# A ring of left operands with 2560 bytes a tile instead of 2112, and small tiles in a pool that closes early

## The chip, the cores and the metric

The kernel runs on one core of one Trainium2 chip. The metric is the device time of one execution in microseconds (us). Times that are compared are medians of several executions on the same chip.

## The reference

One decoder block on 1024 tokens of width 1024, in float32: an RMSNorm, one wide projection, two recurrent mixers side by side (a Mamba-2 scan and gated linear attention), a gated merge, cross-attention on 256 memory tokens, a SwiGLU feed-forward part with an inner width of 2816, and a last RMSNorm. Cut to what matters:

```
proj   = rmsnorm(h) @ w_in                     # 1024 x 7712
y_ssd  = ssd_mixer(z, xBC, dt, ...)            # conv, chunked scan, gated norm
y_gla  = gla_mixer(q, k, v, r, a1, ...)
merged = sigmoid(g_ssd) * (y_ssd @ w_up_ssd) + sigmoid(g_gla) * (y_gla @ w_up_gla)
h      = h + merged @ w_o
h      = h + cross_attention(rmsnorm(h), rmsnorm(mem)) # w_xq, w_xkv, w_xo
g, u   = split(rmsnorm(h) @ w_ffn_in, 2)
h      = h + (silu(g) * u) @ w_ffn_out
out    = rmsnorm(h)
```

## The kernel before

Every large product is made in float32r with each operand split in two: `hi` is the rounded value, written by ScalarE, and `lo` is the rest, written by VectorE or GpSimd (`split`, L221). A product is then three matmuls: hi by hi, hi by lo and lo by hi.

The projection and the gate and up halves of the feed-forward part go through `Unit` objects (L275). One unit covers 256 columns of the weight matrix and all tokens, as a two by two block scheme with seven products instead of eight (`B11`, `B21`, `T1`, `B22`, `T2`, `T3`, `T4`). `Unit.step` (L320) makes one of the seven: it takes a 128x512 left block (a block of the raw weights, or a sum of blocks in `sa`), takes a pair of tiles from the ring `wring`, splits the block into them, and issues 12 matmuls, four blocks of the inner dimension by three. In these matmuls the left operand is the stationary one (128x128, loaded into TensorE before the matmul), and the right operand is the moving one (128x512, streamed through). The right operands (`B11h`, `B11l`, `T1h` and so on) are made once by `Operands` (L230) and lie in slots of 8192 bytes a partition in the pools `sl0op` and `sl1aux`; the results `o` and the raw weights lie in such slots too.

```
def wring():                                              # L225
    hi = wp.tile([P, 528], F32R, name="whi", tag="whi", bufs=3)
    lo = wp.tile([P, 528], F32R, name="wlo", tag="wlo", bufs=3)
    return hi, lo
...
for k in range(kh):                                       # in Unit.step, L341
    for x, y in ((wh, xh), (wh, xl), (wl, xh)):
        PE.matmul(p[:, cs], x[:, k, :], y[:, k, cs], ...)
```

The helper's `PE.matmul` stands on L51, so all matmuls carry that line, and all `tensor_tensor` operations of the helpers stand on L73. The first matmul of a list such as (wh, xh), (wh, xl), (wl, xh) has `x` as stationary and `y` as moving operand.

The ring has three tiles `whi` and three `wlo`. A unit uses 512 of a tile's 528 columns. Two other users take them: `kv_unit` (L549) uses 512 columns for the memory keys and values, and `v_steps` (L636) uses all 528, as two blocks of 264 columns, as moving operands.

The other dense products do not use the ring. `dense` (L1176) takes left operands from two slots named `wd` (the five matrices w_up_ssd, w_up_gla, w_o, w_xq, w_xo) and right operands `hl`, all of them in slots. The last stage, with w_ffn_out, takes both operands from slots named `fs`. Attention takes keys and values from slots named `kvhl`.

A tile pool gives each tile a fixed place in SBUF, one pool behind the other: `const`, the ring, the 14 `op` slots, the 4 `aux` slots, two tiles `sa`, and behind these the pools of one stage after the other (`vp` and `stg`; `gprep`; `conv`; `ssd`; `gla`; then the 4 `m` slots, `res` and `sa2`), which take the same room in turn. A tile in that room waits for the last users of what lay there. The scheduler sets the order of instructions; hints of priority (`ahead`) draw the splits and the evacuations of PSUM forward.

The stages in order of time: memory keys and values, x and the v columns (0 to about 200 us); the z columns with the preparation of the scans, then the convolution's units (to about 400); r, q, k and the first gate columns beside the Mamba-2 scan (to about 620); gate columns beside gated linear attention (to about 840); the five dense products with attention (to about 1340); the gate and up units (1350 to 1800); the w_ffn_out product (to the end).

Of the kernel before, what the change touches and what calls it, by code (L numbers as in the profile page):

```python
# [9 lines left out]
F32 = mybir.dt.float32  # L10
F32R = mybir.dt.float32r
# [5 lines left out]
P = 128  # L17
# [4 lines left out]
MEM = 256  # L22
# [7 lines left out]
NCH = TOK // CH  # L30
NH = 16
# [47 lines left out]
def block_kernel(ctx: ExitStack, tc: tile.TileContext, t: dict, out: bass.AP):  # L79
# [10 lines left out]
    def pool(name, bufs=1, space=None, stack=None):  # L90
        kw = {"reuse_waits": "tile"} if space is None else {"space": space}
        return (stack or ctx).enter_context(tc.tile_pool(name=name, bufs=bufs, **kw))

    cp = pool("const")
    dr = pool("dram", 1, bass.MemoryType.DRAM)
    wp = pool("w", 3)
# [42 lines left out]
    def open_slots(key, n, stack):  # L139
        slots[key] = (pool(f"sl{len(slots)}{key}", n, stack=stack), n)  # L140
# [5 lines left out]
    open_slots("op", 14, opst)  # L146
    open_slots("aux", 4, auxst)
    sums = {"aux": pool("sa0", 2, stack=auxst)}

    st1 = ExitStack()  # L150
    vp = pool("vp", 1, stack=st1)
# [54 lines left out]
    def rsqrt(o, v, scale):  # L206

        DVE.tensor_scalar(o, v, scale, EPS, ALU.mult, ALU.add)
        POOL.tensor_tensor(o, o, mhalf[:, :o.shape[1]], ALU.pow)
# [13 lines left out]
        sub(e or DVE, lo, src, hi)  # L223

    def wring():  # L225
        hi = wp.tile([P, 528], F32R, name="whi", tag="whi", bufs=3)
        lo = wp.tile([P, 528], F32R, name="wlo", tag="wlo", bufs=3)
        return hi, lo

    class Operands:  # L230

# [43 lines left out]
    class Unit:  # L275
# [44 lines left out]
        def step(s, name, B, cs=ALL, again=False):  # L320
            s.load()
            kh = s.kh
            if name == "B11":
                s.banks, s.swap, s.u = {}, B.swap, False
                s.out()
            if again:
                wh, wl = s.w
            else:
                with ahead():
                    src = s.left(name)  # L330
                    hi, lo = wring()
                    s.w = wh, wl = [x[:, :kh * P].rearrange("p (k c) -> p k c", c=P) for x in (hi, lo)]
                    split(src, wh, wl)
            xh, xl = B[name]
            key = s.BANK[name]
            fresh = key not in s.banks
            if fresh:
                s.banks[key] = acc()
            p = s.banks[key]
            m = 0  # L340
            for k in range(kh):  # L341
                for x, y in ((wh, xh), (wh, xl), (wl, xh)):
                    PE.matmul(p[:, cs], x[:, k, :], y[:, k, cs], start=fresh and m == 0, stop=m == 3 * kh - 1,
                              skip_group_check=True)
                    m += 1
            s.evac(name, p, cs)
# [106 lines left out]
    def drain(g):  # L453
        for _ in g:
            pass
# [88 lines left out]
    for a in range(2):  # L544
        ACT.activation(msq, wide(mt[:, a]), AF.Square, accum_out=mss[:, a:a + 1])
    rsqrt(mss, mss, 1.0 / D)
    mbc = cp.tile([P, MEM], F32, name="mbc")

    def kv_unit(c0):  # L549

# [6 lines left out]
        for kk in range(4):  # L557
            with ahead():
                hi, lo = wring()
                hv = hi[:, :512].rearrange("p (k c) -> p k c", c=256)  # L560
                lv = lo[:, :512].rearrange("p (k c) -> p k c", c=256)
                split(raw[:, 2 * kk:2 * kk + 2, :], hv, lv, either(lo))
            for i in range(2):
                o = pa[i][:, :256]
                for k2 in range(2):
                    k = 2 * kk + k2
                    for m, (x, y) in enumerate(((hv, mh), (lv, mh), (hv, ml))):
                        w_, m_ = x[:, k2, :], y[:, k, :]
                        if c0 < D:
                            PE.matmul(o, w_[:, i * P:(i + 1) * P], m_, start=k == 0 and m == 0, stop=k == 7 and m == 2)  # L570
                        else:
                            PE.matmul(o, m_[:, i * P:(i + 1) * P], w_, start=k == 0 and m == 0, stop=k == 7 and m == 2)
            yield
# [41 lines left out]
    w_in = t["w_in"]  # L615


    dt_t = cp.tile([P, NCH, NH], F32, name="dt_t")
    a1_t = cp.tile([P, NCH, NH], F32, name="a1_t")
    HW = 264  # L620

    vraw = {}
# [13 lines left out]
    def v_steps():  # L636
        for pr in range(2):
# [13 lines left out]
            for n, name in enumerate(CHAIN):  # L651
                parts = []
                with ahead():
                    e = either(A11, 2.0)
                    if name == "T1":
                        add(e, sa, A21, A22)
                    elif name == "B22":
                        sub(e, sa, sa, A11)
                        sub(either(A11, 2.0), A12, A12, sa)
                    elif name == "T3":  # L660
                        sub(e, A21, A11, A21)
                    a = (A11, A12, sa, A12, sa, A21, A22)[n]
                    for k2 in range(2):
                        hi, lo = wring()
                        hv, lv = hi.rearrange("p (k c) -> p k c", c=HW), lo.rearrange("p (k c) -> p k c", c=HW)
                        split(a[:, 2 * k2:2 * k2 + 2, :], hv, lv)
                        parts.append((hv, lv))
# [46 lines left out]

    st2 = ExitStack()
    gp = pool("gprep", 1, stack=st2)
    cs = cp.tile([P, P], F32, name="cs")
    dec = cp.tile([P, P], F32, name="dec")
    ec = cp.tile([P, P], F32, name="ec")
    dtv = cp.tile([P, NCH, NH], F32, name="dtv")  # L720
    ebm = cp.tile([P, 4, NCH], F32, name="ebm")
    ebl = cp.tile([P, 4, NCH], F32, name="ebl")
    ewl = cp.tile([P, 4, NCH], F32, name="ewl")

    def conv(u, unit):
        cv = cvp.tile([P, 2, TOK], F32, name="cv", tag="cv", bufs=2)
# [377 lines left out]
    run(singles(gs[1:] + gg[:3], B, gg[3:]), (gla, 8 * 5 / 36), prio=PRIO)  # L1104
    drain(gla)
    st4.close()


    st5 = ExitStack()
# [110 lines left out]
    def presum():  # L1220


        r = slot("m", (P, 2, D), name="pre")
        for k in range(KP):
            SP.dma_start(r, t["w_ffn_out"][256 * k:256 * k + 256, :].rearrange("(j p) c -> p j c", p=P))
            yield
            a = lambda i, j: r[:, j, half(i)]
            s1_ = sums["m"].tile([P, HALF], F32, name="sa", tag="sa", bufs=2)
            put = lambda n, ap: SP.dma_start(down_d[(n * KP + k) * P:(n * KP + k + 1) * P, :], ap)
            e = lambda: either(s1_, 1.0)  # L1230
            add(e(), s1_, a(1, 0), a(1, 1))
            put(0, s1_)
            yield
            sub(e(), a(1, 1), s1_, a(0, 0))
            put(1, a(1, 1))
            yield
            sub(e(), a(1, 0), a(0, 0), a(1, 0))
            put(2, a(1, 0))
            yield
            sub(e(), a(0, 1), a(0, 1), a(1, 1))  # L1240
            put(3, a(0, 1))
            yield
# [48 lines left out]
    early = presum()  # L1291
# [301 lines left out]
    for x, (n, k, kn) in enumerate(todo):  # L1593
        name = CHAIN[n]
# [4 lines left out]
        cs = slice(0, 256) if n == 6 else ALL  # L1599
# [9 lines left out]
    cs = slice(256, 512)  # L1609
# [43 lines left out]
```

## Time and profile before

| | |
|---|---|
| time, median of 3 runs | 2020.93 us (2019.97 to 2023.35) |
| profiled execution | 2021.46 us, of which span 2019.7 us |
| mean granted TensorE clock | 0.994 |
| TensorE matmuls | busy 97% of the span |
| VectorE / ScalarE / GpSimd | busy 65% / 43% / 33% |
| DMA | 309.59 MB, mean 153 GB/s |

The span runs from the first to the last instruction. PE stands for TensorE's matmuls and PEld for its loads of stationary operands, which run beside the matmuls; DVE is VectorE, ACT is ScalarE, POOL is GpSimd, SP is the engine whose queue issues the DMAs. Matmuls overlap in the pipeline, and their ends are modelled, so the time of one (about 390 ns in the groups) is a latency. What a matmul costs is the distance from its start to the next one's start. Where the chain of the profile merges a run of matmuls that follow each other without a wait, that distance is the length of the piece divided by the number in it.

### The profile page before, as it was taken

How to read it: one execution, taken by the hardware profiler on the slowest of the kernel's cores; microseconds unless marked ns; L12 is line 12 of the kernel's file. 1: busy time of each engine (PE TensorE's matmuls, PEld its weight loads, DVE VectorE, ACT ScalarE, POOL GpSimd, SP SyncE). 2: the span in 40 equal slices, each digit the busy share in tenths (PEclk: the TensorE clock that was granted, in tenths of full speed). 3: DMA queues.
4: the chain of work that ended last, by engine and by line, in shares of the span. 5: the costliest groups of instructions: out<-in, count | busy, mean ns of one | idle time of the engine just before them, and what ended most of it. 6: DMA issues, size and time to landing. Idle time of an engine off the chain costs nothing.

```text
span 2019.7 us, 26310 instructions
## 1 busy us (share of the span) xinstructions
PE 1951.1 (97%) x9772; PEld 1616.6 (80%) x9772; DVE 1314.3 (65%) x1869; ACT 861.4 (43%) x1482; POOL 658.6 (33%) x482
## 2 busy tenths in 40 slices
PE   7899999999999989999999999999999999999998
PEld 7798678877777778787778888877888888887887
DVE  6866679879986656532444227478777777774565
ACT  7434745465552455432233226453333333354243
POOL 3521343355653212023322100255444444430002
PEclk9899999999999999999999999999999999999999
DMA  9332232356553655797773210433224223276463
GB/s 308 133 117 98 97 121 105 123 180 190 168 168 107 211 160 177 249 356 247 283 238 132 79 42 22 138 126 107 79 89 136 89 82 114 77 258 221 149 228 128
DMA packets 240724, 309.59 MB, mean 153 GB/s; under 512 B 16443, under 2 KB 164133, under 8 KB 240597
## 3 DMA queue, kind: packets, MB, share of 16 engines
q1 hardware_dynamic: 240596, 307.92, 45.6%
q8 instruction: 77, 1.26, 0.3%
q14 instruction: 51, 0.41, 0.1%
HBM read 211.07 MB, written 96.80 MB: 152 GB/s over the span
## 4 chain that ended last, share of the span: by engine, by line
PE 46%; DMA 6%; DVE 4%; issue 3%; ACT 2%; POOL 1%; SPq 0%; POOLq 0%; ACTq 0%; DVEq 0%
PE acc L51 41%; PE bank L51 5%; DMA gates<-gg_d 2%; DMA ysg_d<-gates 1%; PE bank L55 1%; DMA gates<-gs_d 1%; POOL pre L73 1%; DVE fs L73 1%; DMA down_d<-pre 1%; DMA fr<-act_d 1%; DMA pre<-in_w_ffn_out_dram 1%; DVE hl L73 1%; DVE gates L73 1%; DMA hl<-ys_d 0%; POOL ssum L73 0%
## 5 line engine op out<-in xcount | busy, mean ns | idle before, releaser
L51 PE MATMUL acc<-hl,wd 128*128 128x512 f32 x1920 | 442.2, 390 | 8.4 <-ACT wd L222 4.4
L51 PEld LDWEIGHTS acc<-hl,wd 128*128 128x128 f32 x1920 | 359.2, 188 | 87.3 <-ACT wd L222 6.1
L73 DVE TENSOR_TENSOR wlo<-raw,whi 128x512 fp32r<-128x512 f32 x264 | 242.6, 923 | 78.1 <-ACT whi L222 77.8
L222 ACT ACTIVATE whi<-raw 128x512 fp32r<-128x512 f32 x272 | 170.1, 629 | 249.9 <-PE acc L51 223.4
L73 DVE TENSOR_TENSOR o<-acc,o 128x512 f32<-128x512 f32 (+1 forms) x256 | 172.7, 676 | 112.9 <-PE acc L51 99.2
L51 PE MATMUL acc<-fs 128*128 128x512 f32 (+1 forms) x792 | 156.0, 356 | 1.6 <-ACT o L1548 1.5
L51 PEld LDWEIGHTS acc<-fs 128*128 128x128 f32 x792 | 130.6, 189 | 22.7 <-ACT o L1548 1.9
L73 POOL TENSOR_TENSOR raw<-raw,sa 128x512 f32<-128x512 f32 x48 | 65.5, 1364 | 252.9 <-DVE wlo L73 249.7
L222 ACT ACTIVATE fs<-fr 128x1024 fp32r<-128x1024 f32 (+1 forms) x84 | 80.0, 985 | 112.9 <-PE acc L51 39.7
L73 DVE TENSOR_TENSOR fs<-fr,fs 128x1024 fp32r<-128x1024 f32 (+1 forms) x84 | 99.8, 1218 | 38.7 <-ACT fs L222 38.1
L73 DVE TENSOR_TENSOR wd<-raw,wd 128x1024 fp32r<-128x1024 f32 x40 | 50.4, 1261 | 86.8 <-ACT wd L222 86.6
L222 ACT ACTIVATE whi<-sa 128x512 fp32r<-128x512 f32 x96 | 60.0, 626 | 103.5 <-PE acc L51 103.2
L73 POOL TENSOR_TENSOR sa<-raw 128x512 f32<-128x512 f32 x47 | 73.4, 1562 | 84.7 <-DMA raw<-in_w_in_dram 47.3
L73 DVE TENSOR_TENSOR wlo<-sa,whi 128x512 fp32r<-128x512 f32 x96 | 83.1, 865 | 23.6 <-ACT whi L222 22.1
L73 POOL TENSOR_TENSOR raw<-raw 128x512 f32<-128x512 f32 x48 | 82.8, 1725 | 4.9 <-DVE sa L73 4.9
L73 POOL TENSOR_TENSOR ssum<-ssum,sq 128x512 f32<-128x512 f32 (+1 forms) x23 | 35.2, 1532 | 147.5 <-ACT sq L489 143.6
L51 PE MATMUL acc<-B21h,whi 128*128 128x512 f32 x192 | 77.4, 403 | 2.9 <-ACT o L352 2.9
L73 POOL TENSOR_TENSOR o<-o 128x512 f32<-128x512 f32 x29 | 49.3, 1704 | 91.3 <-DVE o L73 81.0
L51 PE MATMUL acc<-B11h,whi 128*128 128x512 f32 x192 | 76.2, 397 | 2.3 <-ACT whi L222 2.3
L51 PE MATMUL acc<-T1h,whi 128*128 128x512 f32 x192 | 76.4, 398 | 1.4 <-ACT whi L222 1.4
L51 PE MATMUL acc<-T2h,whi 128*128 128x512 f32 x192 | 76.2, 397 | 1.5 <-ACT whi L222 1.5
L51 PE MATMUL acc<-T4h,whi 128*128 128x512 f32 x192 | 76.7, 399 | 1.1 <-DVE o L73 1.1
(376 smaller groups left out, 4798.4 us busy)
## 6 DMA issues: line engine op xcount, KB each, us to landing
raw<-in_w_in_dram SPq DMA_DIRECT2D x26, 1024.0 KB, 6.5
raw<-in_w_ffn_in_dram SPq DMA_DIRECT2D x22, 1024.0 KB, 7.7
act_d<-o SPq DMA_DIRECT2D x77, 256.0 KB, 2.3
fr<-act_d SPq DMA_DIRECT2D x35, 512.0 KB, 4.8
pre<-in_w_ffn_out_dram SPq DMA_DIRECT2D x11, 1024.0 KB, 6.0
fr<-down_d SPq DMA_DIRECT2D x20, 512.0 KB
down_d<-pre SPq DMA_DIRECT2D x33, 256.0 KB, 3.3
raw<-in_w_xkv_dram SPq DMA_DIRECT2D x8, 1024.0 KB
```

Of the source, the lines that this page charges most:

```text
L51: return s.e.matmul(o, x, y, **kw)
L55: return s.e.transpose(o, x, i)
L73: return f(*a, **kw)
L222: ACT.activation(hi, src, AF.Copy)
```

## The change

The ring's tiles become 640 columns wide, 2560 bytes a partition, of which the kernel uses the first 528 as before. Ten small tiles (`mbc`, `dt_t`, `a1_t`, `cs`, `dec`, `ec`, `dtv`, `ebm`, `ebl`, `ewl`, together 4480 bytes) move from the pool `const`, which stays for the whole kernel and lies ahead of the ring, to a new pool `early` behind `sa`, which is closed when gated linear attention is done.

```
-        hi = wp.tile([P, 528], F32R, name="whi", tag="whi", bufs=3)
-        lo = wp.tile([P, 528], F32R, name="wlo", tag="wlo", bufs=3)
-        return hi, lo
+        return [wp.tile([P, 640], F32R, name=n, tag=n, bufs=3)[:, :528] for n in ("whi", "wlo")]
...
     sums = {"aux": pool("sa0", 2, stack=auxst)}
+    st_early = ExitStack()
+    ep = pool("early", 1, stack=st_early)
...
-    mbc = cp.tile([P, MEM], F32, name="mbc")
+    mbc = ep.tile([P, MEM], F32, name="mbc")
...
-    cs = cp.tile([P, P], F32, name="cs")
+    cs = ep.tile([P, P], F32, name="cs")
...
     drain(gla)
     st4.close()
+    st_early.close()
```

The other eight small tiles change from `cp.tile` to `ep.tile` in the same way. In the built programs the tiles begin at these bytes of a partition (behind the stroke the rest on division by 512):

| | before | after |
|---|---|---|
| whi | 9696/480, 11808/32, 13920/96 | 5216/96, 7776/96, 10336/96 |
| wlo | 16032/160, 18144/224, 20256/288 | 12896/96, 15456/96, 18016/96 |
| slots op, aux, m | all rest 352 | all rest 96 |
| sa, first stage pool | rest 352, 173920/352 | rest 96, 176608/480 |

A step of `k` in a unit is 512 bytes in the left operand and 2048 in the right one, so the rests hold for all 12 matmuls of a product. In the tiles of `v_steps` the second block of 264 columns begins 1056 bytes, 32 more than twice 512, behind the first.

Every engine's instructions are the same and stand in the same order before and after. The waits differ in a few instructions where the dense products begin.

More of the change, by code (lines that the diff above doesn't have):

```diff
@@ L615, in block_kernel @@
     w_in = t["w_in"]
-    dt_t = cp.tile([P, NCH, NH], F32, name="dt_t")
-    a1_t = cp.tile([P, NCH, NH], F32, name="a1_t")
+    dt_t = ep.tile([P, NCH, NH], F32, name="dt_t")
+    a1_t = ep.tile([P, NCH, NH], F32, name="a1_t")
     HW = 264
@@ L716, in block_kernel @@
     gp = pool("gprep", 1, stack=st2)
-    cs = cp.tile([P, P], F32, name="cs")
[L718 to L723, printed above, removed]
+    cs = ep.tile([P, P], F32, name="cs")
+    dec = ep.tile([P, P], F32, name="dec")
+    ec = ep.tile([P, P], F32, name="ec")
+    dtv = ep.tile([P, NCH, NH], F32, name="dtv")
+    ebm = ep.tile([P, 4, NCH], F32, name="ebm")
+    ebl = ep.tile([P, 4, NCH], F32, name="ebl")
+    ewl = ep.tile([P, 4, NCH], F32, name="ewl")
     def conv(u, unit):
```

## The prediction

> **What bounds the kernel now.** I read the busy shares first, then a table of 100 us stretches, then the chain of work that ended last, and last the waits of TensorE's matmuls stage by stage. The page's first part has an engine's busy time, its share of the span and its instructions:
>
> ```profile
> PE 1951.1 (97%) x9772; PEld 1616.6 (80%) x9772; DVE 1314.3 (65%) x1869; ACT 861.4 (43%) x1482; POOL 658.6 (33%) x482
> ```
>
> TensorE is the engine to watch, but being busy 97% only says that it rarely has nothing in flight. The stretches show whether another engine is near its own limit where the ring is used (two of the scan, one of the convolution, one of the gate and up units; start:end, length, then busy time of each engine, clock and DMA share):
>
> ```profile
> core 0: us, PE busy (x) PEld busy (x) DVE busy (x) ACT busy (x) POOL busy (x), PEclk, DMA share, GB/s
> 300.00:400.00 100.00, 100.00 (x431) 80.30 (x431) 90.96 (x93) 50.59 (x66) 37.90 (x22) 1.00 0.33 114
> 400.00:500.00 100.00, 96.67 (x606) 77.62 (x605) 83.81 (x143) 55.93 (x125) 50.35 (x39) 1.00 0.59 183
> 500.00:600.00 100.00, 96.54 (x620) 78.81 (x619) 86.10 (x154) 55.93 (x125) 59.65 (x45) 1.00 0.60 181
> 1400.00:1500.00 100.00, 100.00 (x433) 81.06 (x432) 74.75 (x94) 34.12 (x59) 45.36 (x31) 1.00 0.34 111
> ```
>
> TensorE has the full clock in all four and work in flight nearly all the time; VectorE is next, closest at 91% in the convolution. So here the rate at which matmuls start sets the pace. The chain gives that rate, since it merges matmuls that follow each other without a wait (start, length, count):
>
> ```profile
> 1032.72 103.20 PE acc L51 x454
> ...
> 1139.68 68.62 PE acc L51 x302
> ...
> 1273.34 72.77 PE acc L51 x321
> ...
> 1387.80 391.98 PE acc L51 x1691
> ...
> 1849.99 50.09 PE bank L51 x221
> ```
>
> All are float32r matmuls of 128x512. The first three pieces are dense products (`wd` by `hl`): 103.20/454 = 227.3 ns, 68.62/302 = 227.2, 72.77/321 = 226.7. The last is the w_ffn_out product (`fs` by `fs`): 226.7. Together 294.68/1298 = 227.0 ns. The fourth is the gate and up stage, all of it ring products: 391.98/1691 = 231.8 ns. Shape and clock are the same, and no wait of the matmul queue falls in these pieces. The difference is 4.8 ns a matmul, 2.1%.
>
> What differs is where the operands lie. In the four fast pieces both come from slots, with the same rest 352 at 512 bytes; in the slow piece the left one comes from the ring with the rests 480, 32, 96, 160, 224 and 288. Which two operands meet, the timeline shows (start, length):
>
> ```profile
> 1500.07 0.39 PE L51 MATMUL acc<-T2h,wlo 128*128 128x512 f32 x1
> 1500.08 0.19 PEld L51 LDWEIGHTS acc<-T2h,whi 128*128 128x128 f32 x1
> ...
> 1500.30 0.39 PE L51 MATMUL acc<-T2h,whi 128*128 128x512 f32 x1
> 1500.31 0.19 PEld L51 LDWEIGHTS acc<-T2l,whi 128*128 128x128 f32 x1
> ```
>
> While a matmul streams its right operand, TensorE loads the next matmul's left operand, from 10 ns after the matmul's start and for 0.19 of the 0.23 us. So both reads run side by side nearly all the time, and a clash of their addresses would cost in every matmul. Sorted by the offset between the streamed operand and the one being loaded, the starts behind the ring's matmuls have means of 229.2 to 234.1 ns for all twelve offsets that occur at 1024 bytes, and the slots' 227.0 and 226.9 for offsets 0 and 512; the pieces above are the grouped rows of both.
>
> [...]
>
> **The change part by part.** *The ring's rest.* After the change all operands of all units have rest 96, so each streamed and each loaded operand lie a multiple of 512 apart. The number of matmuls this touches follows from the units: each loads its weights once, and makes 7 products of 12 matmuls.
>
> ```profile
> raw<-in_w_in_dram SPq DMA_DIRECT2D x26, 1024.0 KB, 6.5
> raw<-in_w_ffn_in_dram SPq DMA_DIRECT2D x22, 1024.0 KB, 7.7
> ...
> L51 PE MATMUL acc<-B11h,whi 128*128 128x512 f32 x192 | 76.2, 397 | 2.3 <-ACT whi L222 2.3
> ```
>
> 48 units by 84 are 4032 (as 21 such groups of 192). At 231.8 - 227.0 = 4.77 ns each that is 19.2 us, 8.8 of them in the 22 feed-forward units (1848 matmuls) and 10.4 in the other 26 (2184). I take the fast pieces' 227.0 for the rate after: they are the nearest rows, three different left and right tiles, all with offset 0. The ends for this term: nothing, if the offset isn't the cause, and 19.2.
>
> *What of it reaches the end.* In the gate and up stage all of it, since a piece of 392 us has no wait. In the scans and attention stages some matmuls wait for other engines; a TensorE that arrives sooner then waits longer. The waits of TensorE, from 400 to 620 us, then from 620 to 830, then from 1350 to 1800 (total, times, longest):
>
> ```profile
> PE bank L51 <- DVE y L73: 3.3, 4, 1.1
> PE bank L51 <- DVE diag L73: 2.0, 3, 1.1
> PE acc L51 <- ACT whi L222: 1.7, 2, 1.2
> ...
> PE bank L55 <- ACT o L1063: 4.5, 3, 1.9
> PE bank L51 <- DVE attm L73: 2.5, 3, 1.1
> ...
> PE acc L51 <- ACT o L352: 2.1, 1, 2.1
> PE acc L51 <- DVE wlo L73: 1.4, 2, 0.9
> ```
>
> In the two mixer stretches TensorE waits some 15 times in the rows shown, mostly for steps of the scans. Those stretches hold r, q, k and the gates less the last unit, some 15 units: 1260 matmuls, 6.0 us of the gain. If every step of the scan were late anyway all of it would go; the steps themselves begin at matmuls that also come sooner, so none need go. I take a third, 2.0 us. In the convolution VectorE would go from 91% to 93% (90.96 by 231.8/227.0), still short of full, so I take nothing there.
>
> *Narrow matmuls of the ring.* `v_steps` and `kv_unit` have 264 and 256 columns. The first of them:
>
> ```profile
> 139.83 0.28 PE L51 MATMUL acc<-whi,B21h 128*128 128x264 f32 x1
> 139.95 0.28 PE L51 MATMUL acc<-whi,B21l 128*128 128x264 f32 x1
> ...
> 140.67 0.41 PE L51 MATMUL acc<-wlo,B21h 128*128 128x264 f32 x2
> 140.91 0.28 PE L51 MATMUL acc<-whi,B21h 128*128 128x264 f32 x1
> ```
>
> Nine distances in 1.08 us are 120 ns; 227.0 scaled to 264 columns would be 117. With 2 pairs of columns by 7 products by 48 matmuls, 672, at 3 ns that is at most 2.0 us, of which half can't come, since the second block of 264 columns keeps an odd rest. I take nothing and keep 2.0 as an end.
>
> *The splits.* Their three operands now have equal rests too. VectorE on `o`, whose operands always had, beside a split from `sa`:
>
> ```profile
> L73 DVE TENSOR_TENSOR o<-o 128x512 f32<-128x512 f32 x75 | 54.5, 728 | 2.9 <-POOL B21l L73 1.2 <-ACT o L1443 1.0
> L73 DVE TENSOR_TENSOR wlo<-sa,whi 128x512 fp32r<-128x512 f32 x96 | 83.1, 865 | 23.6 <-ACT whi L222 22.1 <-issue 1.3
> ```
>
> Equal rests cost VectorE nothing in 728 ns beside 865. I take nothing either way.
>
> *The early pool.* No instruction is added or moved, DMAs included. The first loads of `gates` wait for one store of `yg_d` less, the first load of yg_d takes that wait, and the first addition of the w_ffn_out sums (`sa` from `pre`) waits for the end of linear attention as well:
>
> ```profile
> SPq L1254 <- DMA yg_d<-sr: 2.9, 1, 2.9
> ...
> POOL sa L73 <- DMA pre<-in_w_ffn_out_dram: 31.3, 1, 31.3
> ```
>
> Two rows later in the same queue the 2.9 us wait comes back, and GpSimd's addition waits 31.3 us for a DMA that lands after linear attention's last transposes, so both cost nothing; TensorE waits for neither in the first dense product. Ends: 2.9 us on each side.
>
> The sum: 19.2 - 2.0 = 17.2 us less. Against the profiled execution, 2021.46 us (its span of 2019.7 and 1.8 around it), that is 2004.3. The median of the runs stands 0.5 below that execution, so I forecast 2003.8.
>
> **The rivals.** *Half is handed back.* If VectorE's scan steps and the convolution take all that TensorE gains outside the feed-forward units, only 8.8 us stay: 2020.9 - 8.8 = 2012. For it: VectorE at 84 to 91% there. Against it: the waits in those stretches are few and short, and 91% still leaves 9 us in 100 for 2 us more.
>
> *The offset isn't the cause.* The ring's tiles are written by ACT and DVE a few us before use, in pairs, for every 12 matmuls; the slower starts might belong to that rhythm. Then nothing moves: 2021, within 3 us. [...] Against it: the `fs` tiles are written shortly before use as well and run at 226.7 ns, and the starts differ by offset within one stage.
>
> *Slower: it is the place, not the distance.* In all fast pieces the left operand has the rest 352 itself, and no ring tile has it. If the rate hangs on where the left operand begins, the change takes 352 from `wd` and `fs`, gives them 96, which the third ring tile has now among the slow ones, and leaves the ring slow:
>
> ```profile
> L51 PE MATMUL acc<-hl,wd 128*128 128x512 f32 x1920 | 442.2, 390 | 8.4 <-ACT wd L222 4.4 <-DVE wd L73 2.9 <-DVE o L73 0.9
> L51 PE MATMUL acc<-fs 128*128 128x512 f32 x528 | 122.5, 391 | 1.5 <-ACT o L1548 1.5
> L51 PE MATMUL bank<-fs 128*128 128x512 f32 x264 | 60.0, 389 | 0.0
> ```
>
> 2712 matmuls by 4.77 ns are 12.9 us more: 2034. It decides from the point where rest 96 is as slow on its own as the ring is now. Against it: a left operand's step of 512 bytes crosses 512 byte lines alike at 352 and at 96, and two reads side by side make a distance the simpler cause.
>
> **How the numbers follow.** The forecast has 0.75, half handed back 0.12, no effect 0.09, slower 0.04. The forecast's own range is 2000 to 2008: the full 19.2 and the 2.0 of the narrow matmuls below, all 6.0 of the mixer stretches lost above. The range given reaches up to the second case, 1999 to 2012.5, and leaves out some 0.15. A change of 0.2%, 4 us, is about what a measurement of this kernel can tell from none, the three runs being 3.4 us apart. Faster: 0.75 + 0.12 = 0.87; the same: 0.09; slower: 0.04.
>
> **What the profile after would show.** If the step on the rate is right, the merged piece of the gate and up stage has 227 ns a matmul, 100 us there hold 440 matmuls in place of 433, and the dense pieces stay at 227. If they go to 232, the third rival holds. If TensorE's waits from 400 to 830 us grow by more than 2 us, the loss there was put too low. What would make the prediction wrong is above all a gate and up stage that still starts a matmul every 231.8 ns.

## The result and the profile after

The changed kernel takes 2007.49 us (median of 6 runs, 2006.73 to 2008.78) beside 2020.54 for the kernel before in the same rounds: a ratio of 0.9937, with a 95% interval of 0.9923 to 0.9952. That is 13.0 us less; the forecast was 2003.8 us, where the sum had taken off 17.2. The profiled execution has a span of 2006.1 us, 13.6 less than before.

The chain of work that ended last, after, with the pieces that stand in the prediction for before (start, length, count):

```profile
1025.88 103.20 PE acc L51 x454
...
1132.84 68.62 PE acc L51 x302
...
1266.54 72.77 PE acc L51 x321
...
1381.08 383.36 PE acc L51 x1691
...
1804.57 31.84 PE acc L51 x132
1836.41 59.84 PE bank L51 x264
```

The dense pieces have their old lengths to 0.01 us. The gate and up piece goes from 391.98 to 383.36 us for the same 1691 matmuls: 226.7 ns each instead of 231.8, as fast as the slots. The starts also tell where the time went. The first dense piece begins 6.84 us sooner than before and the gate and up piece 6.72 sooner; that stage gains 8.6 more. Then 1.6 us are lost at once: the piece of 132 matmuls, the first of the w_ffn_out product, has 31.84 us now, and had before:

```profile
1819.78 30.21 PE acc L51 x132
```

The stretches of the prediction, after:

```profile
300.00:400.00 100.00, 99.03 (x431) 80.23 (x430) 90.62 (x92) 49.31 (x66) 37.86 (x22) 1.00 0.33 113
400.00:500.00 100.00, 96.51 (x610) 77.92 (x609) 84.52 (x144) 57.73 (x130) 51.85 (x39) 1.00 0.60 184
500.00:600.00 100.00, 96.39 (x634) 78.62 (x634) 85.94 (x155) 56.23 (x122) 60.12 (x45) 1.00 0.58 175
1400.00:1500.00 100.00, 100.00 (x443) 82.80 (x442) 77.39 (x93) 35.02 (x60) 50.29 (x34) 1.00 0.27 91
```

The gate and up stage has 443 matmuls in 100 us for 433. The convolution (first row) has 431, exactly as before: nothing was gained there, and TensorE is no longer in flight all the time (99.03). The waits of TensorE from 290 to 385 us, which were none before, are now

```profile
PE acc L51 <- DVE wlo L73: 1.0, 5, 0.2
```

once in each unit. The timeline, from B22 in one unit to B22 in the next, shows what such a wait costs (start, length, then the idle time as the view sees it):

```profile
296.34 0.39 PE L51 MATMUL acc<-B22h,whi 128*128 128x512 f32 x1
296.56 0.39 PE L51 MATMUL acc<-B22l,whi 128*128 128x512 f32 x1
297.16 0.50 PE L51 MATMUL acc<-B22h,wlo 128*128 128x512 f32 x1 [0.21 <-DVE wlo L73]
297.50 0.39 PE L51 MATMUL acc<-B22h,whi 128*128 128x512 f32 x1
...
315.88 0.39 PE L51 MATMUL acc<-B22h,whi 128*128 128x512 f32 x1
```

From 296.56 to 297.50 two start-to-start distances take 0.94 us where 0.45 would do, and the unit's period is 19.54 us (315.88 - 296.34), though 84 matmuls at 226.7 ns are 19.04.

### The profile page after: what moved, and what is told of

Same layout as the page of the kernel before. It is cut to its first block, busy times and chain, and to the rows that moved or that the text cites. A ratio compares the mean times of both kernels' runs of the same rounds, so it can differ in the third digit from the quotient of the medians.

```text
span 2006.1 us, 26309 instructions
## 1 busy us (share of the span) xinstructions
PE 1940.5 (97%) x9772; PEld 1622.2 (81%) x9772; DVE 1312.7 (65%) x1869; ACT 859.6 (43%) x1482; POOL 658.8 (33%) x482
## 4 chain that ended last, share of the span: by engine, by line
PE 44%; DVE 2%; DMA 2%; issue 1%; POOL 1%; ACT 1%; SPq 0%; POOLq 0%; DVEq 0%; ACTq 0%
PE acc L51 39%; PE bank L51 4%; DMA pre<-in_w_ffn_out_dram 1%; DMA fr<-act_d 1%; DVE fs L73 1%; POOL pre L73 1%; PE bank L55 0%; DMA down_d<-pre 0%; POOL ssum L73 0%; POOL sa L73 0%; DVE o L73 0%; DVE wlo L73 0%; DVE T2l L73 0%; ACT fs L224 0%; DVE phl L73 0%
## 5 line engine op out<-in xcount | busy, mean ns | idle before, releaser
L51 PE MATMUL acc<-B22h,wlo 128*128 128x512 f32 x192 | 77.1, 402 | 1.2 <-DVE wlo L73 1.2
```

What stands on the lines that cost most here:

```text
L51: return s.e.matmul(o, x, y, **kw)
```

## The experiments

Each was run beside the kernel before on the same chip; ratios are to that.

**The pool alone.** The changed kernel with the ring's old tiles:

```
-  [wp.tile([P, 640], F32R, name=n, tag=n, bufs=3)[:, :528] ...]
+  [wp.tile([P, 528], F32R, name=n, tag=n, bufs=3)[:, :528] ...]
```

> The early pool without the wider ring: the ring's tiles keep 2112 bytes, so the offsets between streamed and loaded operands are the same six rests as before (128 to 448), while all tiles lie lower. Theory A (the distance of the two operands sets the rate): the merged piece of the gate and up stage stays at 231.8 ns a matmul, 392 us for 1691, and the time is that of before, 2020 us within 4. Theory B (the pool's move, with its other waits and places, brings the gain): about 2007 us and 227 ns.

Measured: ratio 0.9988 (0.9977 to 0.9999), 2017.17 beside 2019.22 us, and

```profile
1384.05 391.98 PE acc L51 x1691
```

That is 231.8 ns, and the piece's length of before to the hundredth, although the ring and the slots lie elsewhere than before. Theory B falls: the pool's move and its other waits do not bring the rate; it changed only when the ring's rests did.

**One distance that is no multiple of 512.** A tile that nothing uses stands between the ring and the slots; everything else is the changed kernel.

```
     wp = pool("w", 3)
+    pad = pool("pad").tile([P, 64], F32, name="pad")    # 256 bytes; 16: 64 bytes; 32: 128; 112: 448
```

> The changed kernel with 256 unused bytes between the ring and the slots: all six ring tiles have one and the same rest, 256 away from that of the right operands. Theory A (the distance must be a multiple of 512): 231 to 234 ns a matmul in the gate and up stage as for that offset before, 390 to 396 us for 1691, and a time of 2018 to 2026 us. Theory C (any distance will do as long as it is the same from matmul to matmul, so that the two reads keep one phase): 227 ns, 383 us, 2007 us.

> The changed kernel with 64 unused bytes between the ring and the slots: one distance of 448 for all ring matmuls. Theory A: between 229 and 231 ns, the mean that this offset had before, so 387 to 391 us for 1691 matmuls and 2012 to 2019 us. Theory C (a constant distance is enough): 227 ns, 383 us, 2007 us.

> 128 unused bytes between the ring and the slots, so one distance of 384 for all ring matmuls. Theory C in its pure form (a constant distance is enough): 226.7 ns and 383.4 us for 1691. Theory F (a price for each distance, by which 448 costs 2.2 ns): with 128 as a divisor still free 226.7, else 228 to 233 ns, as this offset had 233.5 in the mixed ring.

> 448 unused bytes between the ring and the slots: one distance of 64 for all ring matmuls. If the price is alike on both sides of a multiple of 256, as for 192 or 448: 228.9 ns, 387 us for 1691. If not, the price lies anywhere from 226.7 to the 232.4 of the distance 384, and tells with the other four what the mixed ring's mean would be without a price for changes: three pairs of tiles, distances 128 and 64, 192 and 128, 256 and 192 at 512, the first of each pair used twice as often.

A distance is the loaded operand's address less that of the streamed one, its rest on division by 512. Measured, the same merged piece of the chain of each, for 256 bytes:

```profile
1382.30 383.36 PE acc L51 x1691
```

for 64 bytes (distance 448):

```profile
1386.46 387.08 PE acc L51 x1691
```

for 128 bytes (distance 384):

```profile
1386.45 392.97 PE acc L51 x1691
```

and for 448 bytes (distance 64):

```profile
1383.86 394.58 PE acc L51 x1691
```

| distance at 512 | ns a matmul (length/1691) | time, us | ratio to before |
|---|---|---|---|
| 0 (the changed kernel) | 226.7 | 2007.49 | 0.9937 (0.9923 to 0.9952) |
| 256 | 226.7 | 2006.96 | 0.9936 (0.9920 to 0.9951) |
| 448 | 228.9 | 2011.85 | 0.9960 (0.9946 to 0.9974) |
| 384 | 232.4 | 2021.04, one run | |
| 64 | 233.3 | 2020.02, one run | |

Theory A in the form "a multiple of 512" falls with the second row, and theory C (any constant distance) with the last three. A constant distance has a price: nothing at 0 and 256, and 2.2 to 6.6 ns at the three others, dearer 64 above a multiple of 512 (6.6) than 64 below (2.2).

One rival is left in these rows: the unused tile moves the slots, so the rest of the right operand changes as well as the distance. The dense products settle it, since both of their operands lie in slots: with the slots at the rests 160, 224 and 32 (the rows 448, 384 and 64) the dense piece of 321 matmuls takes 72.77, 72.78 and 72.77 us, as before. The place alone costs nothing.

**Two distances in turn.** The high halves at distance 0, the low ones at another: the ring is opened as two pools with the unused tile between them.

```
+    wp = {"whi": pool("w", 3)}
+    pad = pool("pad").tile([P, 64], F32, name="pad")    # 256 bytes; 48: 192 bytes
+    wp["wlo"] = pool("w2", 3)
+    pad2 = pool("pad2").tile([P, 64], F32, name="pad2") # 256 bytes; 80: 320 bytes
```

> The high halves of the ring stay a multiple of 512 from the right operands, the low halves lie 256 further. Both distances gave 226.7 ns a matmul when they were the only one. Theory C (what costs is a distance that changes from one matmul to the next): 229 to 233 ns in the gate and up stage, 388 us or more for 1691 matmuls. Theory F (each distance has a price of its own, and 0 and 256 have none): 226.7 ns, 383.4 us.

> High halves of the ring a multiple of 512 from the right operands, low halves 192 further. Theory F (each distance has a price of its own; 448 alone had 2.2 ns, which is 192 on division by 256): one matmul in three pays, 0 to 3 ns on the mean, 226.7 to 228 ns in the gate and up stage, 383 to 386 us for 1691. Theory C' (a price by distance and another for each change of the distance between matmuls, as the mixed ring's 231.8 with its 64 to 192 suggests): 229 ns or more, over 387 us.

Measured, 0 and 256 in turn (2005.58 us in its one run):

```profile
1380.65 383.36 PE acc L51 x1691
```

and 0 and 192 in turn (2015.24 us in one run):

```profile
1382.49 391.20 PE acc L51 x1691
```

226.7 and 231.3 ns. For a rule by 256 bytes, 0 and 256 are one distance, so the first says little on theory C and fits F. For the second, take prices to repeat every 256 bytes, which only 0 and 256 show; then 192 costs the 2.2 ns of distance 448, and one matmul in three at that price would make 227.4. The remaining 3.9 ns fit theory C', a price for changing the distance from matmul to matmul. The distance 192 was not run alone, but to explain the 231.3 by itself it would have to cost 13.8 ns, twice the dearest price measured. The trace points the same way, though a delay that carries over to the next matmul is not excluded: while a low half is loaded, at distance 192, the matmuls start 230.4 ns apart, and while the two high halves are loaded, at distance 0, 233.8 and 229.9. The ring before mixed 64, 128, 192 and 0 at 256 bytes; prices by distance alone would give it 230.1 ((2 x 5.7 + 6.6 + 2 x 2.2 + 5.7 + 2.2)/9 = 3.4 ns over 226.7), and it had 231.8.

**What the convolution lost.** Two kernels, one with the wide and one with the old ring, leave out one of the three shifted taps of the convolution's sum, which eases VectorE:

```
-            for m in range(3):
+            for m in range(2):
```

> The changed kernel with two of the convolution's three shifted taps on VectorE, so 12 operations of about 1.1 to 2 us less; the second shifted tap is left out of the sum. Theory D (VectorE and GpSimd, late with the left block of B22, ended the period of a unit in the convolution): the five waits for the low half at B22 go, and the five periods of 19.5 us fall to 84 x 227 ns = 19.1 us. Rival G (the loss in the convolution lies in matmuls that start slowly there, not in waits): the waits and periods stay.

> The early pool with the ring's old 2112 bytes, and two taps in place of three (the second shifted tap left out). Theory D: with VectorE eased, TensorE alone sets the convolution, so each period is 84 x 231.8 = 19.5 us, 0.4 longer than with the wide ring and two taps; over five units the wide ring gains 2 us there, where with three taps it gained 0.1. Rival G: both rings keep the same period here too.

Measured from 300 to 380 us, the wide ring first, then the old one (columns as in the stretches above):

```profile
300.00:380.00 80.00, 80.00 (x354) 66.26 (x354) 55.02 (x68) 40.79 (x54) 27.28 (x16) 1.00 0.34 119
```

```profile
300.00:380.00 80.00, 80.00 (x347) 64.85 (x346) 57.03 (x66) 40.13 (x53) 27.73 (x16) 1.00 0.32 111
```

With three taps both rings have 345 there, the old ring (the kernel before) first:

```profile
300.00:380.00 80.00, 80.00 (x345) 64.25 (x345) 72.72 (x74) 40.12 (x53) 29.57 (x16) 1.00 0.32 111
```

```profile
300.00:380.00 80.00, 79.22 (x345) 64.19 (x344) 72.71 (x74) 40.67 (x54) 29.55 (x16) 1.00 0.33 114
```

With VectorE eased, neither waits, and the wide ring makes 354 matmuls where the old one makes 347: 2.0%, close to the 2.2% of the gate and up stage. The starts of B22 are 19.04 us apart with the wide ring, 84 x 226.7 ns exactly, and 19.44 to 19.49 with the old one. Theory D holds: what VectorE has to finish there took the gain. The whole time of the first, 2011.05 us in one run, is not below the changed kernel's. In its trace it reaches the first 512-column matmul of the units 3.9 us behind the changed kernel (175.45 and 171.51 us), is level with it at the end of the convolution, and is 3.3 us behind again at the first dense product (844.58 and 841.26); what lost the time at these two places was not tried.

**Other orders of work in the convolution.** B22 put last among the products of a unit that is worked alone, in the convolution and in all other such units:

```
-SPACED = ("B11", "T2", "T1", "B21", "T3", "B22", "T4")
+SPACED = ("B11", "T2", "T1", "B21", "T3", "T4", "B22")
```

> The changed kernel with B22 and T4 exchanged in the order of the seven products of a single unit, so that the block that needs three additions on GpSimd comes last. Theory D (in the convolution the gain is lost since TensorE now waits for the low half of B22's left block, 0.37 us and the slow matmul behind it in each of five units): these waits go, and the time falls by 2 to 3 us to about 2005. Rival E (VectorE is full there): the waits move to another product of the same unit, the period of 19.5 us stays and the time with it, 2007.

Measured: ratio 1.0001 (0.9988 to 1.0014), 2019.54 us: all of the gain gone. TensorE's waits from 290 to 385 us, which were 1.0 us in five:

```profile
PE acc L51 <- DVE wlo L73: 4.0, 5, 0.8
```

Both expectations missed it: the waits neither went nor stayed, they grew from 0.2 to as much as 0.8 us each, and the unit's period from 19.6 to 20.1 or 20.2 us. The rest of the loss lies outside the convolution, as in a wait of 3.8 us for the low half at 236 us, ahead of it.

The next one moves the units' sums from GpSimd to VectorE, since GpSimd's chain ahead of B22 was long and VectorE's split took up to 1785 ns where its median is 684. In the changed kernel, 282 to 399 us (count, then shortest/median/longest ns):

```profile
L73 POOL TENSOR_TENSOR sa<-raw x6: 2260/2267/2267, 290.4 to 388.2; 128x512 f32<-128x512 f32 x6
L73 POOL TENSOR_TENSOR sa<-sa,raw x6: 1627/1629/1629, 292.7 to 390.5; 128x512 f32<-128x512 f32 x6
L73 POOL TENSOR_TENSOR raw<-raw x6: 2276/2286/2286, 294.3 to 392.1; 128x512 f32<-128x512 f32 x6
```

```profile
L73 DVE TENSOR_TENSOR wlo<-raw,whi x30: 675/684/1785, 288.3 to 396.0; 128x512 fp32r<-128x512 f32 x30
```

Of these 30 splits, the 17 with no GpSimd operation beside them take 675 to 684 ns, and 12 of the other 13 take 1773 to 1785; VectorE's `o<-acc,o` keeps 678 to 683 beside GpSimd.

```
-            e = either(A11, 2.0)
+            e = DVE if s.dve else either(A11, 2.0)      # s.dve for the six convolution units
...
-                sub(either(A11, 2.0), A12, A12, s.S2)
+                sub(e, A12, A12, s.S2)
```

> The changed kernel, with the sums of left blocks of the six convolution units on VectorE instead of GpSimd (four of 128x512 a unit, 1.3 to 2.3 us each on GpSimd, 0.68 us unhindered on VectorE). If the late left block of B22 is GpSimd's chain of 2.3, 1.6 and 2.3 us, and VectorE's own operations take 1 us longer each time GpSimd reads beside them, both go: no wait at B22, five periods of 19.1 us instead of 19.5, and 2 us less than the changed kernel, 2005. If VectorE has no time left for 2.7 us a unit more, the waits grow and the time is 2009 or more.

Measured, 300 to 380 us:

```profile
300.00:380.00 80.00, 79.78 (x352) 65.72 (x351) 71.34 (x89) 41.04 (x55) 5.73 (x3) 1.00 0.34 115
```

The convolution does gain: 352 matmuls, periods of 19.04 us for most units, and no more VectorE time than before in spite of four additions more a unit (71.34 us for 72.71). Yet the time is 2011.2 us, ratio 0.9952 (0.9939 to 0.9966). By 700 us TensorE was 3.4 us ahead of the changed kernel, and 4.0 at 990; at 1010 us it was 5.4 behind, mostly by one wait of 5.8 us in the dense products. From 690 to 1050 us, where the changed kernel has 2.5 us in two such waits:

```profile
PE acc L51 <- ACT wd L224: 7.3, 2, 5.8
```

The clock fell behind that wait as well (the columns are start:end, length, PE busy, clock, DMA share and GB/s):

```profile
1000.00:1015.00 15.00, 9.15 (x32) 0.77 0.66 232
```

There the w_ffn_out sums and the gates' loads share SP's queue, and ScalarE, which splits the next left operand, stood behind a load of `gates` for up to 10.4 us. Whether a sooner start makes that meeting worse or it was chance was not tried.

**The first matmuls behind an interruption.** One extra transposition in each product of the gate and up stage:

```
+                if k == 1 and s.W is t["w_ffn_in"]:
+                    PE.transpose(bank()[:, :P], wh[:, k, :].bitcast(F32), ident)
```

> The changed kernel with one extra transposition of 128x128 inside each of the 154 products of the gate and up stage (its result isn't used), so that runs of ring matmuls are cut every 13 matmuls on the mean. Theory H (after an interruption the two reads start out of step, and the wide ring needs about nine matmuls to come to 226.7 ns): the first matmuls behind a transposition start 228 to 234 ns apart, the stage's mean rises to 228.5 to 230, and the stage grows by 154 x 0.11 = 17 us for the transpositions and 3 to 5 us more. Rival I (the slow matmuls behind the waits of the scan stages belong to what goes on in those stages): the distances stay at 226.7 between two transpositions, and the stage grows by 17 us alone.

Measured, some uninterrupted pieces of the chain:

```profile
1393.36 5.50 PE acc L51 x24
...
1401.82 3.68 PE acc L51 x16
...
1408.46 2.77 PE acc L51 x12
...
1413.41 6.40 PE acc L51 x28
```

These are 18.35 us for 80 matmuls, 229.4 ns each, where the unbroken stage has 226.7. Over the stage the mean distance is about 228.6. Behind the first matmul, whose start belongs to the transposition, it is about 231.5 for three, 227 to 230 up to the ninth, and 226.7 from the tenth on. From its first ring matmul to the first of the w_ffn_out product the stage takes 447.5 us instead of 426.7, 20.8 more; the transpositions are 17 of it (154 by 0.11 us). The times are those of theory H, and rival I falls. That the two reads are out of step until then, as theory H has it, is argued and was not seen.

## Why the prediction was right, and where it was off

*The rate.* The forecast of 227.0 ns for ring matmuls at a distance of 0 holds where they run unbroken (226.7), and the feed-forward units gained what the sum gave them: from the first ring matmul to the w_ffn_out product 435.4 us before and 426.7 now, 8.7 for a forecast 8.8. The stage has the 443 matmuls in 100 us that the rate asks for.

*The cause.* That the distance does it is shown: kernels that differ in nothing but the size of an unused tile differ by 11.2 us over the same 1691 matmuls (394.58 and 383.36), and the dense pieces of the same kernels do not differ. Why a distance has its price stays open. The prediction's "multiple of 512" was narrower than need be: 256 does as well (226.7 ns at both).

*The convolution: the step that failed.* The prediction took nothing off there since VectorE would be busy 93% and not full. The gain of 0.4 us a unit was lost whole, 2.4 us over six. The mean share was the wrong test: TensorE waits for one late chain in each period (three sums on GpSimd, a split, VectorE's low half), and that chain had no slack left at the old rate already: before the change six loads of a stationary operand waited 1.5 us in all for these low halves, without a wait of a matmul, and the unit's period was 19.49 to 19.60 us, where one tap less gave the old ring 19.44 to 19.49. The rival "half is handed back" was right about this place.

*The mixer stretches.* The term was 2.0 us lost of 6.0. From the end of the convolution to the first dense matmuls 2.7 us were gained, so 3.3 were lost. TensorE's named waits did not grow (400 to 620 us: the 3.3, 2.0 and 1.7 of before are 3.2, 2.0 and 1.6). What was missing in the sum is the slow restart: these stretches cut the ring's runs with scan matmuls, and their ring matmuls that wait for nothing still start 227.5 to 229.2 ns apart in stretches of 100 us. Behind an interruption they have the steps of the last experiment: 232.0, 232.4 and 231.3 ns for the first three distances, 227 to 231 up to the ninth, 226.7 from the tenth. Together the distances lay 5.2 us above 227.0 ns each before, and lie 1.3 above now.

The clock fell here too, where the kernel before has 1.00 from 680 to 695 us. The changed kernel:

```profile
680.00:695.00 15.00, 11.83 (x48) 0.77 0.69 216
```

With a wait of 2.1 us ahead of it, TensorE went from 4.5 us ahead of the kernel before (at 682 us) to 0.4 ahead (at 695). By 720 us it was 4.5 ahead again, since two waits of 1.9 and 1.1 us that the kernel before has there were gone. So this fall cost nothing in the end.

*Stage borders.* Between the first dense matmuls and the gate and up stage 2.0 us were gained that the sum did not have: TensorE's waits for `wd` there went from 7.3 (4.4 and 2.9) to 4.7 us (2.5 and 2.2). This was luck: from these matmuls (851 us in the changed kernel) to the first of the gate and up stage the kernel before takes 494.2 us and the changed one 492.3, and the others, with slow rings and fast ones, take 489.6 to 495.4 (499.1 with the convolution's sums on VectorE). And 1.6 us were lost at the start of the w_ffn_out product, where the granted clock fell. The changed kernel, then the kernel with distances 0 and 256, in the same stretch:

```profile
1800.00:1815.00 15.00, 13.16 (x52) 0.89 0.65 232
```

```profile
1800.00:1815.00 15.00, 13.33 (x60) 1.00 0.60 217
```

From 1805.5 to 1808.0 us the granted clock is 0.50 and the matmuls start 426 to 427 ns apart; 0.89 over 15 us is 3.3 us at that clock, to the rounding of 0.89. Before the change (1815 to 1830 us) and in the second kernel the clock was 1.00 at that place. With the one distance of 256 the 132 matmuls have 31.81 us as well, so the loss does not hang on a distance of 0. TensorE stood idle for 1.84 us of this stretch, ahead of the fall, and for 1.67 in the second kernel, where none came; what brings the fall was not shown.

Together: 17.2 forecast, less 2.4 in the convolution, 1.3 more than the 2.0 in the mixer stretches and 1.6 for the clock, and 2.0 gained in the dense products, make 13.9 for the 13.6 found. It fits so well partly by chance, and not in the dense products alone. For the five units ahead of the convolution the sum had 2.0 us, and TensorE is 2.1 ahead where the convolution begins; but 0.9 of it was there at these units' first matmul (172.46 us before, 171.51 after), which the other kernels reach anywhere from 171.2 to 175.5 us.

*The rest.* The splits, the narrow matmuls and the early pool were put at nothing; the pool alone has a ratio of 0.9988, within the 0.2% that tell nothing. The third rival, that the left operand's own place sets the rate, falls with the dense pieces, which have 103.20 us for 454 at the rest 352 and at 96, and with the ring, which is fast at the rest 96.

## What to carry to other kernels

Where matmuls run back to back, take the start-to-start distance from the longest merged pieces and compare stages of the same shape: a difference of 2% that no wait explains (here 231.8 and 226.7 ns) can lie in addresses. For float32r matmuls of this shape, give the tiles that are loaded and the tiles that are streamed the same rest on division by 256, for all tiles of a ring: here 226.7 ns at the distances 0 and 256, and 228.9 to 233.3 at the three others. Then ask of each stage not how busy the next engine is, but which chain arrives last in a period: in the convolution it took the whole gain, 2.4 us.

## What the runs showed of the hardware

- With a stationary 128x128 float32r operand and a moving 128x512 one, the time of a matmul changed with the distance of their addresses: 226.7 ns at 0 and 256 bytes, 228.9 at 448, 232.4 at 384, 233.3 at 64.
- Distances that change from matmul to matmul seem to cost more than their parts: 0 and 192 in turn have 231.3 ns, where 226.7 for 0 and, as an estimate for 192, the 228.9 of 448 would give 227.4. The distance 192 alone was not run.
- At the distance 0 the rate of 226.7 ns is reached only after some nine matmuls in a row; until then a matmul costs 227 to 232 ns, behind an extra transposition in the gate and up stage and behind the scans' matmuls alike.
- The splits hardly changed with the rests. Over the whole kernel VectorE's low halves have means of 923 ns (from `raw`) and 865 (from `sa`) with the old ring, and 930 and 865 with the new one; ScalarE's high halves 629 and 626, and 628 and 626. In the gate and up stage alone VectorE's medians moved both ways (721 to 916 from `raw`, 1360 to 1020 from `sa`), and what moved them was not tried.
